# Sums of squares of norms: tiles added on GpSimd first, and summed over the partitions by TensorE once a norm

## The chip, the core and the metric

The kernel runs on one core of a Trainium2 chip. The metric is the device time of one execution in microseconds (us), as a median over runs. Engines are named as the profile names them: PE is TensorE (PEld its weight loads), DVE is VectorE, ACT is ScalarE, POOL is GpSimd, SP is SyncE, which issues most of the DMAs.

## What is computed

The reference is a network of two blocks over 256 tokens of 1024 features. The first block has a recurrent mixer (RWKV and S5) and a feed-forward. The second has two layers, each with gated linear attention, latent attention, a convolution module and a convolutional feed-forward; in its first layer 256 context tokens go along. What matters here are the norms between these parts:

```python
def _layer_norm(x, g, b):
    mu = x.mean(-1)
    var = ((x - mu) ** 2).mean(-1)
    return (x - mu) * rsqrt(var + eps) * g + b

def _rms_norm(x, g):
    return x * rsqrt((x * x).mean(-1) + eps) * g

x = _layer_norm(DN_ALPHA * x + gate1 * y, ln1_g, ln1_b)          # in every layer, for x and the context
h = silu(_layer_norm(_depthwise_conv(h), conv_ln_g, conv_ln_b))  # convolution module
of = of * rsqrt((of * of).mean(-1) + eps)                        # heads of the gated linear attention
cq, ckv = _rms_norm(pt[6], mla_q_norm), _rms_norm(pt[7], mla_kv_norm)   # latents
```

Each of them needs, for every token, a sum of squares over the features.

## The kernel before

**Layout.** Activations lie with their features on the partitions: a tensor of 1024 features is eight tiles [128 features, tokens], with 256 tokens, or 512 where the first layer of the second block takes x and the context together. So a sum over the features runs over the partitions and over the tiles. Weights are streamed from DRAM in pieces of 512 KB (`wraw`), and each is split into a high part `wh` (ACT, L275) and a low part `wl` (DVE, L276); a k-tile of a product is three matmuls (L311, L312, L313).

**Norms.** For each feature tile ACT squares it, and `colsum` takes the square as the stationary operand, 128 tokens at a time, against a column of ones: a matmul of 128x1 whose sums gather in PSUM (`pc`, in the buffers `aux`) over the tiles. In float32 each of these matmuls is two passes in the trace. `rms_of` then makes 1 / sqrt of the sums on DVE (L372 and eleven small instructions, tiles `rsv`, `rsw`, `rsy`) and spreads the result over the partitions with a transpose on PE (`rowcast`, L367). The places are these:

- Block 1: `post` twice (squares L542, of `b` tiles, as the tiles of a dense product come), and the norm ahead of the feed-forward (`squares`, L521).
- `ln`, six calls: for each feature tile DVE takes off the mean (L1104), ACT squares into an `lt` tile (four buffers, L1106). In layer 0 the norm after the mixer and that after the feed-forward are taken in two parts, of x and of the context; layer 1 has one after the mixer and the final one.
- `conv_norm`, one call a layer: tiles are fetched from DRAM (`od`) into `cv` buffers (two in layer 0, three in layer 1), the mean is taken off (L1406), squared in place (L1407). Its results `yc` (L306, L307) go into the products with `w_conv`.
- The heads of the gated linear attention, four a layer: two tiles each (`ring`, squares L1595).
- `latent`, four calls: two or three tiles each (`pr`).

**Order.** A framework of tiles allots the buffers and puts in the waits. A scheduler fixes the order of each engine's instructions when the program is built, from work that the code offers in steps (`beside()` and the generators of `dense_steps`); on the chip each engine goes through its own list in order. So PE's list mixes matmuls of products with column sums of a norm, and a column sum that isn't ready holds up what stands behind it. GpSimd does four memsets at the start and nothing else.

Of the kernel before, what the change touches and what calls it, by code (L numbers as in the profile page):

```python
# [21 lines left out]
P = 128  # L22
D = 1024
# [11 lines left out]
TAPS = ((5,), (1, 4))  # tiles whose taps the convolution takes at once  # L35
ADA = (17, 1, 1)  # chunks of the modulation beside the recurrence, the feed-forward and the inputs of the layers
# [3 lines left out]
# ------------------------------------------------------------------ host layout  # L40


class Weights:
    """Blocks [128, k-tiles * columns] of up to SPLIT elements a partition, one after the other in one flat array per weight."""
# [4 lines left out]
    def add(self, name, w, groups, moving=False):  # L49
        """w [K, N]; groups: column lists (-1: zeros), one chunk each; blocks of all columns (moving), else of whole tiles  # L50
        of 128 columns"""
# [30 lines left out]
class Vecs:  # L82
    """Per-feature vectors side by side: feature f of a vector -> partition f % 128, column f // 128."""
# [27 lines left out]
def actT(x):  # L111
    """[tokens, D] -> [128, D/128 * tokens]"""
    x = np.asarray(x)
    t, d = x.shape
    return np.ascontiguousarray(x.T.reshape(d // P, P, t).transpose(1, 0, 2).reshape(P, -1))
# [11 lines left out]
def const_arrays():  # L127
# [17 lines left out]
    # RWKV: rows j of a block of 64 steps, columns (a | r) of t  # L145
# [4 lines left out]
    # block levels of the triangular inverse, in A^T [j, t]: j in the even block, t in the odd one  # L150
# [7 lines left out]
    # rope  # L158
# [14 lines left out]
    # swap of the two halves of a 64-block; kr (64 rows) to both halves, straight and swapped  # L173
# [14 lines left out]
# ------------------------------------------------------------------ kernel body  # L188


class Body:
# [24 lines left out]
    def behind(self, work):  # L216
        """work(), whose VectorE instructions go before those of the block"""
# [14 lines left out]
    # ---- constants and vectors  # L232
# [15 lines left out]
    def v(self, which, name):  # L248
        """[128, tiles, L] view of a vector"""
        a, k, L = self.vat[which][name]  # L250
        return self.vt[which][:, a : a + k * L].rearrange("p (k l) -> p k l", l=L)
# [6 lines left out]
    # ---- weights: high and low parts, each exact in float32r  # L258
    def wraws(self, name, ch):
        """the blocks of a chunk as they come, [128, k, c]"""  # L260
# [6 lines left out]
    def wblocks(self, name, ch):  # L267
        """the blocks of a chunk, high and low parts as [128, k, c] each"""
# [10 lines left out]
    def wmoving(self, name, ch):  # L279
        """a chunk as k-tiles (wh, wl) of all its columns"""  # L280
# [4 lines left out]
    def wcols(self, name, ch):  # L285
        """tiles of 128 columns of a chunk, each as k-tiles (wh, wl)"""
# [7 lines left out]
    def split(self, pool, src, shape, tag):  # L294
        """src (float32, SBUF or PSUM) -> high and low parts"""
# [23 lines left out]
    def dense_steps(self, name, chunks, x, epi, tok=None, cuts=()):  # L319
        """epi(m, psum) for each tile m of 128 columns of the chunks, and what it returns one tile later; x: k-tiles  # L320
        [(xh, xl)]; tok: columns of x, by m"""
# [21 lines left out]
    # ---- 1 / sqrt(v), v > 0, small tiles: two steps of third order  # L343
# [14 lines left out]
    def colsum(self, pc, sq, first, last):  # L358
        """pc[:, t] += sum over the features of sq [128, tokens] of token tile t: tokens on partitions"""
# [4 lines left out]

    def rowcast(self, col, t, out):
        """out[p, i] = col[i, t] for every partition p"""
        self.nc.tensor.transpose(out, col[:, t : t + 1].broadcast_to([P, P]), self.ident)  # L367

    def rms_of(self, pc, ntt, dim, eps):
        """psum [128, tokens]: rsqrt(sum / dim + eps) of each token on every partition"""  # L370
# [8 lines left out]
    # ================================================================ block 1  # L379
    def block1(self, X, xp):  # L380
        """X [128, 8, 256], in place"""
# [3 lines left out]
        with ExitStack() as es:  # L385
            bp = es.enter_context(tc.tile_pool(name="b1", bufs=1))
            tp = es.enter_context(tc.tile_pool(name="b1t", bufs=2))
            # ---- pre norm
# [7 lines left out]
            with self.behind(lambda: R.append(self.rms_of(pc, 2, D, EPS))):  # L396
                hh, hl = self.rms_in(bp, X, "norm_mix_pre", R[0])
                # ---- vectors worked out on the chip
# [13 lines left out]
                # ---- projections: r, k, v, (wd | ad), gd with the token shift; u; gates  # L412
# [15 lines left out]
            # gates (twice the sigmoid less one), by way of DRAM  # L428
# [1504 lines left out]
```

## Time and profile before

| what | value |
|---|---|
| median of three runs | 2570.31 us (2566.24, 2570.31, 2585.77) |
| span of the profiled execution | 2588.6 us |
| PE busy | 2504.7 us, 97% |
| DVE, ACT, POOL busy | 1817.3, 1265.6 and 0.2 us (70%, 49%, 0%) |
| mean granted clock of TensorE | 0.971 |

The profiled execution took 18 us longer than the median; its rows give durations and order, and differences worked out from them are taken off the median. A start time in the trace is in us from the beginning of the span. A row of the timeline gives the start, the length, the engine, the line, the operation, the tile written and the tile read, how many instructions it stands for, and in brackets how long the engine had been idle and what ended that.

### The profile page before, as it was taken

The page shows a single profiled execution, that of the slowest core. Times are in us where ns is not written, and L with a number is a line of the kernel's source. Part 1 is how long each engine was busy: PE and PEld are TensorE (multiplying, and loading weights), DVE is VectorE, ACT ScalarE, POOL GpSimd, SP SyncE. Part 2 cuts the span into 40 slices and gives each one's busy share as a digit, 9 for nine tenths or more (in the row PEclk, how much of TensorE's full clock was granted, in tenths as well). Part 3 has the DMA queues.
Part 4 walks back from the last instruction along what each step waited for, and adds up shares of the span by engine and source line. Part 5 has one row for each costly group of instructions (what it writes and reads, how often), then busy time and mean ns, then how long its engine had stood idle before and what let it go on. Part 6 is the DMA issues. An engine that isn't in the chain of part 4 may idle for free.

```text
span 2588.6 us, 46013 instructions
## 1 busy us (share of the span) xinstructions
PE 2504.7 (97%) x18460; PEld 2153.4 (83%) x18460; DVE 1817.3 (70%) x3376; ACT 1265.6 (49%) x2264; POOL 0.2 (0%) x4
## 2 busy tenths in 40 slices
PE   7999998999999999999999999999989999998998
PEld 7587797997788888656888998899978887798998
DVE  8466367864596678778546875656787778877884
ACT  5432245654555542445433654444555545555653
POOL 0000000000000000000000000000000000000000
PEclk9799998999999999999999999999989999998998
DMA  6446565655331223342334452256542332365663
GB/s 212 159 135 234 196 188 172 187 178 170 111 101 52 77 74 97 122 140 87 114 114 154 148 172 97 96 167 186 161 125 87 99 122 80 115 195 164 190 197 111
DMA packets 125781, 361.53 MB, mean 140 GB/s; under 512 B 14208, under 2 KB 39680, under 8 KB 125440
## 3 DMA queue, kind: packets, MB, share of 16 engines
q1 hardware_dynamic: 125568, 358.59, 43.4%
q8 instruction: 145, 2.38, 0.4%
q14 instruction: 68, 0.56, 0.1%
HBM read 344.07 MB, written 14.46 MB: 139 GB/s over the span
## 4 chain that ended last, share of the span: by engine, by line
PE 88%; DVE 6%; ACT 2%; DMA 2%; issue 1%; SPq 0%; ACTq 0%; DVEq 0%
PE mm L311 21%; PE mm L312 21%; PE mm L313 21%; PE aux L362 2%; PE sy L1046 2%; DVE wl L276 2%; PE aux L1711 2%; PE aux L1592 1%; PE sy L1724 1%; PE aux L685 1%; PE aux L1710 1%; PE aux L1548 1%; PE mm L1513 1%; PE mm L1511 1%; PE mm L1512 1%
## 5 line engine op out<-in xcount | busy, mean ns | idle before, releaser
L275 ACT CAST wh<-wraw 128x1024 fp32r<-128x1024 f32 (+3 forms) x544 | 543.5, 1000 | 762.0 <-PE mm L312 640.3
L276 DVE TENSOR_TENSOR wl<-wraw,wh 128x1024 fp32r<-128x1024 f32 (+3 forms) x544 | 631.6, 1162 | 340.6 <-ACT wh L275 335.3
L311 PE MATMUL mm<-hx,wh 128*128 128x256 f32 (+1 forms) x1792 | 609.0, 340 | 13.7 <-ACT hx L303 6.4
L313 PE MATMUL mm<-hx,wl 128*128 128x256 f32 (+1 forms) x1792 | 603.6, 338 | 5.0 <-DVE wl L276 4.8
L312 PE MATMUL mm<-hx,wh 128*128 128x256 f32 (+1 forms) x1792 | 605.6, 339 | 0.2 <-DVE hx L304 0.2
L311 PEld LDWEIGHTS mm<-hx,wh 128*128 128x128 f32 x1792 | 343.1, 192 | 56.1 <-ACT hx L303 7.2
L313 PEld LDWEIGHTS mm<-hx,wl 128*128 128x128 f32 x1792 | 342.2, 191 | 44.5 <-DVE wl L276 6.9
L312 PEld LDWEIGHTS mm<-hx,wh 128*128 128x128 f32 x1792 | 343.3, 192 | 39.7 <-issue 4.7
L1393 DVE SCALAR_TENSOR_TENSOR cv<-u,h_conv_dw,cv 128x512 f32<-128x512 f32 (+1 forms) x480 | 295.2, 615 | 8.6
L311 PE MATMUL mm<-b,wh 128*128 128x256 f32 x688 | 199.5, 292 | 4.2 <-ACT b L303 3.6
L312 PE MATMUL mm<-b,wh 128*128 128x256 f32 x688 | 195.5, 285 | 1.0 <-DVE b L304 1.0
L313 PE MATMUL mm<-b,wl 128*128 128x256 f32 x688 | 195.5, 285 | 0.7 <-DVE wl L276 0.7
L312 PE MATMUL mm<-gx,wh 128*128 128x256 f32 x528 | 148.4, 281 | 0.0
L311 PE MATMUL mm<-gx,wh 128*128 128x256 f32 x528 | 147.8, 280 | 0.0
L313 PE MATMUL mm<-gx,wl 128*128 128x256 f32 x528 | 147.7, 280 | 0.0
L311 PEld LDWEIGHTS mm<-b,wh 128*128 128x128 f32 x688 | 130.8, 191 | 13.1 <-issue 5.3
L312 PE MATMUL mm<-sp,wh 128*128 128x256 f32 (+1 forms) x448 | 141.0, 315 | 0.1
L313 PE MATMUL mm<-sp,wl 128*128 128x256 f32 (+1 forms) x448 | 140.8, 315 | 0.1
L311 PE MATMUL mm<-sp,wh 128*128 128x256 f32 (+1 forms) x448 | 140.7, 315 | 0.0
L313 PEld LDWEIGHTS mm<-b,wl 128*128 128x128 f32 x688 | 131.2, 191 | 5.5 <-issue 2.5
L312 PEld LDWEIGHTS mm<-b,wh 128*128 128x128 f32 x688 | 131.6, 191 | 2.2 <-DVE b L304 1.7
L311 PEld LDWEIGHTS mm<-gx,wh 128*128 128x128 f32 x528 | 99.3, 188 | 0.0
(522 smaller groups left out, 4563.7 us busy)
## 6 DMA issues: line engine op xcount, KB each, us to landing
wraw<-w_up SPq DMA_DIRECT2D x100, 512.0 KB, 3.4
wraw<-w_ada SPq DMA_DIRECT2D x96, 512.0 KB, 4.3
wraw<-w_gates SPq DMA_DIRECT2D x48, 512.0 KB, 3.5
wraw<-w_dn SPq DMA_DIRECT2D x48, 512.0 KB, 3.7
wraw<-f_up SPq DMA_DIRECT2D x44, 512.0 KB, 3.5
wraw<-w_in SPq DMA_DIRECT2D x34, 512.0 KB, 4.1
wraw<-w_conv SPq DMA_DIRECT2D x32, 512.0 KB, 3.8
wraw<-w_o SPq DMA_DIRECT2D x24, 512.0 KB, 3.5
```

Source lines behind the costliest of these rows:

```text
L275: nc.scalar.copy(h, raw)
L276: nc.vector.tensor_tensor(l, raw, h.bitcast(F32), ALU.subtract)
L311: mm(ps, wh, xh, start=first, stop=False)
L312: mm(ps, wh, xl, start=False, stop=False)
L313: mm(ps, wl, xh, start=False, stop=last)
L362: self.nc.tensor.matmul(pc[:, t : t + 1], sq[:, t * P : t * P + P], self.ones[:, 0:1], start=first and t == 0, stop=last and t == n - 1)
L685: mm(ps[q, i], lhs(8 * b + i, q), rhs(8 * b + i, q), start=True, stop=True)
L1046: nc.tensor.matmul(ps[q], self.sc[:, 2 * k : 2 * k + 32], w[:, i], start=k < nt, stop=k >= KT - nt)
L1393: nc.vector.scalar_tensor_tensor(r(o), u[:, :, j : j + S], dw(j), r(o), ALU.mult, ALU.add)
L1511: mm(ps, xh[:, tk], wh, start=kk == 0, stop=False)
L1512: mm(ps, xl[:, tk], wh, start=False, stop=False)
L1711: mm(ps, qr[hs, a], kr[hs, k0:], start=False, stop=True)
```

## The change

A new helper `gather` adds a square to an accumulator with one elementwise instruction on GpSimd. `colsum` is then called once for a norm, on the sum of the tiles. In `squares` and `post` the accumulator is the first square's tile, in `ln` the first `lt` tile, in a head the first square; `conv_norm` gets a tile `acc` of its own in the pool `cp`, and `latent` one in buffers of the tag `vm`. The norm at the head of block 1 is as before.

```diff
+    def gather(self, acc, sq, first):
+        if first:
+            return sq
+        self.nc.gpsimd.tensor_tensor(acc, acc, sq, ALU.add)
+        return acc
...
     def squares(self, pc, X, sq, k):
         self.nc.scalar.activation(sq[:, k], X[:, k], AF.Square)
-        self.colsum(pc, sq[:, k], k == 0, k == KT - 1)
+        self.gather(sq[:, 0], sq[:, k], k == 0)
+        if k == KT - 1:
+            self.colsum(pc, sq[:, 0], True, True)
...
             nc.scalar.activation(sq[:, m], ps, AF.Square, scale=scale)
-            return lambda: self.colsum(pc, sq[:, m], m == 0, m == KT - 1)
+            self.gather(sq[:, 0], sq[:, m], m == 0)
+            if m == KT - 1:
+                return lambda: self.colsum(pc, sq[:, 0], True, True)
...
+        acc = None
         for k in range(KT):
             nc.vector.tensor_tensor(s[k], s[k], R, ALU.add)
             q = self.t(pool, [P, w], tag="lt", bufs=4)
             nc.scalar.activation(q, s[k], AF.Square)
-            self.colsum(pc, q, k == 0, k == KT - 1)
+            acc = self.gather(acc, q, k == 0)
+        self.colsum(pc, acc, True, True)
...
+        acc = self.t(cp, [P, W], tag="acc")
         for k in range(KT):
             o = tile()
             nc.sync.dma_start(o, od[k])
             nc.vector.tensor_tensor(o, o, R, ALU.add)
-            nc.scalar.activation(o, o, AF.Square)
-            self.colsum(pc, o, k == 0, k == KT - 1)
+            q = o if k else acc
+            nc.scalar.activation(q, o, AF.Square)
+            self.gather(acc, q, k == 0)
+        self.colsum(pc, acc, True, True)
...
-            for dv in range(2):
-                self.colsum(pc, sqs[dv], dv == 0, dv == 1)
+            self.colsum(pc, self.gather(*sqs, False), True, True)
...
+            acc = self.t(gp, [P, 4, S], tag="vm", bufs=2).rearrange("p a b -> p (a b)")[:, :w]
...
+                sq = sq if m else acc
                 nc.scalar.activation(sq, t, AF.Square)
                 raw.append(t)
-                return lambda: self.colsum(pc, sq, m == 0, m == kt - 1)
+                self.gather(acc, sq, m == 0)
+                if m == kt - 1:
+                    return lambda: self.colsum(pc, acc, True, True)
```

In all 212 of 276 column-sum matmuls go (two passes each): 28 in the two posts, 14 in the norm ahead of the feed-forward, 84 in the six `ln`, 42 in the two `conv_norm`, 24 in the heads, 20 in the latents. GpSimd gets 91 adds, 76 of 128x256 and 15 of 128x512. ACT, DVE and SP keep their instructions. Lines behind the helper stand 7 to 19 lines lower: L1106, L1407 and L1724 are L1117, L1422 and L1743 after the change.

PE's list in the first part of the norm after layer 0's mixer, before the change (`lt` are the squares, `aux` the sums, `sp` and `wh`, `wl` belong to a product that runs beside the norm):

```order
L312 MATMUL mm_13931<-sp_13531,wh_13927 128x256
L362 MATMUL aux_13833<-v_c_2_75,lt_13851 128x1 x2
L313 MATMUL mm_13931<-sp_13530,wl_13928 128x256
L311 MATMUL mm_13931<-sp_13530,wh_13927 128x256
L312 MATMUL mm_13931<-sp_13531,wh_13927 128x256
L362 MATMUL aux_13833<-v_c_2_75,lt_13856 128x1 x2
```

The same norm after the change:

```order
L311 MATMUL mm_13900<-sp_13470,wh_13896 128x256
L312 MATMUL mm_13900<-sp_13471,wh_13896 128x256
L313 MATMUL mm_13900<-sp_13470,wl_13897 128x256
L311 MATMUL mm_13900<-sp_13470,wh_13896 128x256
L362 MATMUL aux_13773<-v_c_2_75,lt_13776 128x1 x2
L312 MATMUL mm_13900<-sp_13471,wh_13896 128x256
```

The eight pairs have become one, behind 42 matmuls of the product since the mean (L1102), where the last of the eight stood behind 38. In the two parts of the norm after the feed-forward it is 40 for 36 and 45 for 40, in the heads of the linear attention 15 for 10 (layer 0) and 9 for 6 (layer 1), and none for none in the very last head.

ACT's list in the convolution's norm of layer 1, before the change (`cv` are its tiles, `PT`, `pr` and `sy` belong to the latent attention that ends here):

```order
L1407 ACTIVATE cv_22633<-cv_22633 128x256
L1718 ACTIVATE pr_22596,smx_22594<-aux_22590,mx_22593 128x512
L1176 ACTIVATE gate_22945<-mm_22920,h_b_gates_18007 128x256
L275 CAST wh_23015<-wraw_23013 128x1024
L1722 COPY PT_22573<-aux_22600 128x4x128
L1407 ACTIVATE cv_22639<-cv_22639 128x256
L303 CAST sp_21576<-sy_22572 128x256
L1407 ACTIVATE cv_22645<-cv_22645 128x256
```

And after it:

```order
L1741 COPY PT_22478<-aux_22505 128x4x128
L303 CAST sp_21481<-sy_22477 128x256
L1422 ACTIVATE acc_22526<-cv_22527 128x256
L275 CAST wh_22980<-wraw_22978 128x1024
L1189 ACTIVATE gate_22910<-mm_22885,h_b_gates_17926 128x256
L1422 ACTIVATE cv_22541<-cv_22541 128x256
```

The first square, which now writes `acc`, has moved behind the last L303 of the latent attention; the second and third still stand ahead of that. GpSimd's list around the same norm, after the change (there is nothing there before it; `vm` are the accumulators of two latents, `pr` their squares):

```order
L369 TENSOR_TENSOR vm_20705<-vm_20705,pr_20773 128x256
L369 TENSOR_TENSOR vm_20705<-vm_20705,pr_20809 128x256
L369 TENSOR_TENSOR vm_20822<-vm_20822,pr_20890 128x512
L369 TENSOR_TENSOR acc_22526<-acc_22526,cv_22531 128x256
L369 TENSOR_TENSOR acc_22526<-acc_22526,cv_22536 128x256
```

Five more with `acc` follow. Each add reads and writes its accumulator, so that of one norm no add can begin before the one ahead of it has ended, and PE's one pair of column sums waits for the last.

## Rows read from the trace of the kernel before

**Rows 1.** The page: busy time, and the shares of the chain that ended last.

```profile
PE 2504.7 (97%) x18460; PEld 2153.4 (83%) x18460; DVE 1817.3 (70%) x3376; ACT 1265.6 (49%) x2264; POOL 0.2 (0%) x4
...
PE 88%; DVE 6%; ACT 2%; DMA 2%; issue 1%; SPq 0%; ACTq 0%; DVEq 0%
```

**Rows 2.** The column sums' line (L362), those of `ln`: durations in ns, minimum/median/maximum.

```profile
L362 PE MATMUL aux<-v_c,lt x192: 164/250/353, 1424.9 to 2577.9; 128*128 128x1 f32 x192
```

**Rows 3.** Timeline of PE, first part of the norm after layer 0's mixer.

```profile
1428.77 0.28 PE L311 MATMUL mm<-sp,wh 128*128 128x256 f32 x1
1428.89 0.28 PE L312 MATMUL mm<-sp,wh 128*128 128x256 f32 x1
1429.01 0.50 PE L362 MATMUL aux<-v_c,lt 128*128 128x1 f32 x4
1429.37 0.36 PE L313 MATMUL mm<-sp,wl 128*128 128x256 f32 x1
1429.57 0.28 PE L311 MATMUL mm<-sp,wh 128*128 128x256 f32 x1
```

**Rows 4.** Groups by line and form on DVE: busy us, mean ns | idle before.

```profile
L276 DVE TENSOR_TENSOR wl<-wraw,wh 128x1024 fp32r<-128x1024 f32 x472 | 576.9, 1223 | 328.2 <-ACT wh L275 324.0 <-ACT att L1563 1.9
...
L1275 DVE TENSOR_TENSOR ring<-ring,ring 128x512 f32<-128x512 f32 x16 | 11.1, 692 | 0.5
L1247 DVE TENSOR_TENSOR lt<-lt,M 128x256 f32<-128x256 f32 x18 | 7.6, 424 | 0.4
```

**Rows 5.** Timeline of PE, behind the last column sums of a `post`.

```profile
396.62 1.92 PE L1046 MATMUL mm<-wraw,sc 128*32 128x512 f32 x14
```

**Rows 6.** Timeline of DVE, layer 0's convolution norm.

```profile
1249.31 0.69 DVE L1406 TENSOR_TENSOR cv<-cv,sx 128x512 f32<-128x512 f32 x1 [3.37 <-DMA cv<-od]
```

**Rows 7.** Timeline of layer 1's convolution norm, and of the products that take its results.

```profile
2264.34 0.35 ACT L303 CAST sp<-sy 128x256 fp32r<-128x256 f32 x1
...
2271.09 0.16 DVE L372 TENSOR_SCALAR rsv<-aux 128x2 f32<-128x2 f32 x1 [0.56 <-PE aux L362]
...
2318.81 0.28 PE L311 MATMUL mm<-yc,wh 128*128 128x256 f32 x1
...
2319.21 0.43 DVE L307 SCALAR_TENSOR_TENSOR yc<-cv,yc 128x256 fp32r<-128x256 f32 x1 [0.48 <-ACT yc L306]
```

**Rows 8.** Timeline of one head of the linear attention in layer 0, and one in layer 1.

```profile
781.05 0.61 ACT L1595 ACTIVATE ring<-aux 128x512 f32<-128x512 f32 x1
782.46 0.95 PE L362 MATMUL aux<-v_c,ring 128*128 128x1 f32 x8
...
1964.98 0.41 ACT L1595 ACTIVATE ring<-aux 128x256 f32<-128x256 f32 x1
...
1965.74 0.50 PE L362 MATMUL aux<-v_c,ring 128*128 128x1 f32 x4
```

**Rows 9.** Timeline of the first part of the norm after layer 0's mixer: third to seventh square, last column sum.

```profile
1426.73 1.79 ACT L1106 ACTIVATE lt<-M 128x256 f32<-128x256 f32 x5
...
1431.17 0.50 PE L362 MATMUL aux<-v_c,lt 128*128 128x1 f32 x4
```

**Rows 10.** Timeline of three norms: after layer 1's mixer, the final one, ahead of block 1's feed-forward.

```profile
2367.32 2.92 ACT L1106 ACTIVATE lt<-M 128x256 f32<-128x256 f32 x8 [1.62 <-DVE M L1104]
2367.79 4.91 PE L362 MATMUL aux<-v_c,lt 128*128 128x1 f32 x32 [1.33 <-ACT lt L1106]
2372.74 0.16 DVE L372 TENSOR_SCALAR rsv<-aux 128x2 f32<-128x2 f32 x1 [3.13 <-PE aux L362]
...
2570.88 1.88 ACT L1106 ACTIVATE lt<-ring 128x256 f32<-128x256 f32 x5 [9.25 <-DVE ring L1104]
2578.26 0.16 DVE L372 TENSOR_SCALAR rsv<-aux 128x2 f32<-128x2 f32 x1 [5.10 <-PE aux L362]
...
402.27 0.72 ACT L521 ACTIVATE b<-X 128x256 f32<-128x256 f32 x2
404.30 5.28 PE L362 MATMUL aux<-v_c,b 128*128 128x1 f32 x24 [0.51 <-ACT b L521]
409.62 0.16 DVE L372 TENSOR_SCALAR rsv<-aux 128x2 f32<-128x2 f32 x1 [1.96 <-PE aux L362]
```

## The prediction, made before the changed kernel was timed

> **What bounds the kernel now.** I read the page first: PE is busy 97% of the span, and 88% of the chain of waits runs over it [rows 1]. So a matmul taken off PE's list is worth its time wherever PE has other work at hand, and a wait put into that list costs its full length. Then the column sums' own line, which gives their number [rows 2]: 192 passes in the six `ln`, 552 in all by the same count, of which the change leaves 128. The duration printed there (250 ns median) is no price, since matmuls overlap. The price comes from the timeline, where the column sums stand in a row of matmuls: from one L312 to the L311 behind it 0.68 us pass, with four passes and two other matmuls (L312 and L313) in between; two matmuls in a row without column sums are 0.12 us apart. So four passes, a 256-wide tile, add 0.68 − 2 × 0.118 = 0.445 us, 0.111 us a pass, and a 512-wide tile 0.89 [rows 3]. All 424 passes that go are worth 424 × 0.111 = 47 us, 1.8% of the span. This is the ceiling; the question is what the adds on GpSimd give back.
>
> **The price of an add.** No row of before has an elementwise operation on GpSimd. I bound it by DVE's. The same form, float32 with two inputs, takes DVE 0.424 us at 128x256 and 0.692 at 128x512; the nearest row above is 1.223 us for 128x1024, four times the columns [rows 4]. With 0.05 us for the hand-over to the next instruction, the time p from one 256-wide add to the next is between 0.47 (GpSimd as quick as DVE) and 1.27 (it takes for 256 columns what DVE takes for 1024). For 512 columns I call it q: 0.75 to 2.1. I take p = 0.85 and q = 1.4, twice DVE's rows, the middle, because neither end has a row nearer to it. The Trainium skill, page "GPSIMD Engine Reference", section 3.1 (side-by-side cycle accounting), gives a GpSimd add 1.96 times VectorE's time, and section 4.1 puts elementwise adds on VectorE; an estimate by its ratio would be 0.83 and 1.36 without hand-over, and the sum about 2 us less than mine. No run of before shows either.
>
> **Part by part** (gains positive; in brackets the value at the low and at the high end of p). In each norm the adds form a chain, since each reads and writes the accumulator.
>
> *Posts*: two norms, seven tiles' column sums less in each: 2 × 7 × 0.445 = **+6.2** [+6.2, +6.2]. Squares come at the pace of a dense product, slower than the adds at either end, and behind the last square PE still has 14 passes of L1046, 1.92 us, to do [rows 5], which cover the last add.
>
> *Latents*: layer 0 loses three 512-wide tiles, layer 1 two of 256 and one of 512: 4 × 0.89 + 2 × 0.445 = **+4.5** [+4.5, +2.5]. The column sum is queued one tile of the product later, some 24 matmuls or 2.8 us, and square and add together take 0.6 + 1.4. At the high end 0.6 + 2.1 and the waits around them fill this, and up to 0.5 us each is lost.
>
> *Convolution, layer 0*: 7 × 0.89 = 6.2 less on PE. The tiles come through two buffers, which DVE waits for 3.37 us at a time for the load [rows 6]. A buffer is now freed by GpSimd's add and not by PE's, so its round is load 3.2, mean 0.69, square 0.63, add 1.4, together 5.9 us for two tiles, about the pace of before; I leave 1.7 us for PE at the one column sum that is left: **+4.6** [+6.2, +1.9].
>
> *Convolution, layer 1*: here a chain of other engines is late next. The last `yc` is there at 2319.64; PE begins on them at 2318.81 and needs the eighth tile 7 × 3 × 0.118 = 2.5 us later, at 2321.3 [rows 7]. So the norm may come 1.7 us later, no more. The first square writes `acc` and stands behind the L303 that ends at 2264.7; it ends at 2265.1. Its buffer then takes two more tiles (load 3.2, mean and square 0.85, add 0.85 each), the next buffer likewise one add later: the last add ends at 2275.9, and with the column sum and hand-overs L372 runs near 2276.9, 5.8 us after its 2271.09. PE then waits 5.8 − 1.7 = 4.1 us at its first products with `yc`; the 3.1 us of column sums saved earlier only make it wait sooner: **−4.1** [−2.8, −4.7]. If ACT's order were what it was, this term would be about zero.
>
> *Heads*: in layer 0 PE saves eight passes, 0.89 us, and has five more matmuls ahead of its column sum, so it arrives at 782.46 − 0.89 + 5 × 0.118 = 782.16; the second square ends at 781.66, the add 1.45 later at 783.11 [rows 8]. It waits 0.95 and has saved 0.89, four times. In layer 1 the same sum is: arrival 1965.74 − 0.445 + 3 × 0.118 = 1965.65, add done at 1966.27, a wait of 0.62 for 0.445 saved, three times; the last head has no matmul in between and loses 0.4 to 0.5. Together **−1.2** [+3.0, −5.7].
>
> *Three `ln` with a product beside them* (layer 0): 7 × 0.445 = 3.1 us less on PE each. In the one shown the third square is ready at 1427.1, and six adds follow it in a chain: 1427.15 + 6 × 0.85 = 1432.25. PE reaches its column sum at 1431.17 − 3.1 + 4 × 0.118 = 1428.55 [rows 9]. It waits 3.7 us for 3.1 saved; three such norms give 3 × −0.6 = **−1.8** [+4.8, −9.6].
>
> *Four bare norms*, where PE has little else to do and the next step is DVE's L372. In the one after layer 1's mixer the eight squares take 2.92 us and the 32 passes 4.91, so L372 runs at 2372.74. After: second square at 2368.1, seven adds 5.95, column sum and hand-over 0.55: 2374.6, or 1.85 later. The second part of the norm after layer 0's mixer goes alike: 2 × −1.85. In the final norm 32 passes take longer, L372 at 2578.26; after: 2571.65 + 5.95 + 0.85 = 2578.45, −0.2. Ahead of block 1's feed-forward 402.99 + 5.95 + 0.9 = 409.85 against 409.62, −0.2 [rows 10]. Together **−4.1** [+5.2, −15.9].
>
> ACT, DVE and SP keep their work; 91 adds are some 85 us of GpSimd's span, which has nothing else to do.
>
> The **sum**: 6.2 + 4.5 + 4.6 − 4.1 − 1.2 − 1.8 − 4.1 = +4.1 us at p = 0.85; with p at 0.47 it is +27, with p at 1.27 it is −25. So the sign turns near p = 0.91. Measured against the median of 2570.3, not against the profiled execution's 2588.6 us span, whose extra 18 us I can't place in any norm, the forecast is 2566 us. About 1%, 26 us, is what a measurement of this kernel can tell from no change; 4 us is inside.
>
> **The rivals.**
>
> (A) *The gain of PE shows in full as far as chains allow.* If an add takes what DVE's rows show, p = 0.47, all terms but layer 1's convolution are gains: +27, 2543 us. For it speaks that GpSimd has nothing else to do [rows 1]; against it that nothing here shows it to be as quick. One percent is reached below p = 0.5.
>
> (B) *The adds wait for DVE, and PE for the adds: slower than before.* DVE has an instruction with two inputs running most of the time: the split of the weights alone is 472 instructions of 1.223 us, 577 us of the span [rows 4], and it goes on beside the three `ln` and the convolution norms. If an add that arrives during one starts only behind it, p grows from 0.85 by up to 1.22, by 0.6 if it falls anywhere within. The place are PE's column sums in the `ln`, since seven adds follow each other there; at p = 1.27 the sum is −25, 2595 us, and every further 0.1 costs 7 us. It decides from p = 0.91 for the sign. In the bare norms DVE is free for most of the chain, and this speaks for a loss of half that. By the Trainium skill, page "SBUF — State Buffer", section "Who interferes with whom", a VectorE operation with two SBUF inputs and GpSimd exclude each other for the length of an instruction, by a lock on a shared port; the trace of before has no GpSimd instruction beside one of VectorE and shows nothing of it.
>
> (C) *The change doesn't do what it says.* The list of PE has the 212 matmuls fewer, so this is out but for a scheduler that fills the gaps otherwise; a percent at most.
>
> **How the numbers follow.** The forecast, p between 0.5 and 1.2 and little harm from DVE, 2550 to 2590 around 2566: 0.62. (A) 2540 to 2550: 0.12, all but a little of it over 1% faster. (B) from 2590 up, with its half form inside 1%: 0.24. (C) 0.02. The range 2543 to 2598 takes both ends of p and a few us beyond the high one; 2 in 10 stay outside, most of them above. Faster by over 1% is 0.12, as (A); slower by over 1% 0.17, the larger part of (B); the rest, 0.71, within.
>
> **What would show it.** In the profile after, L362 has 128 passes in place of 552. The add's line on GpSimd gives p: mean and pitch, alone (after layer 1's mixer) and beside DVE's L276; a mean that is longer there speaks for (B). PE's idle time ahead of L362 should name the adds and be near 3.7 us in the three `ln` with a product, 0.9 in the heads, none in posts and latents. L372 should run 1.9 us later after the mean in the bare norms. PE should wait some 4 us for `yc` in layer 1. The forecast is wrong if p is outside 0.5 to 1.2, if DVE's instructions grow longer beside the adds (then the weights' low parts come late, and PE waits for `wl`), or if the granted clock falls in PE's new waits and stays low behind them.

## The result, and the profile after

The changed kernel is slower: 2594.43 us against 2574.26 us (medians of 14 runs each), a ratio of 1.0070 with an interval of 1.0053 to 1.0088. By the ratio that is a loss of some 18 us where a gain of 4 was forecast; the time lies inside the stated range, on the other side of no change.

The page of the changed kernel, busy time by engine, to be read against [rows 1]:

```profile
PE 2450.2 (94%) x18036; PEld 2100.6 (81%) x18036; DVE 1823.4 (70%) x3376; ACT 1266.8 (49%) x2264; POOL 86.3 (3%) x95
```

PE has the 424 passes fewer and is busy 54 us less, 43 less than in a second profile of the kernel before that follows below (2493.3 us; the first had TensorE at half clock for a stretch). The time is longer all the same. So the work went, and waits came. The groups of the adds on GpSimd (busy us, mean ns | idle before and what ended it):

```profile
L369 POOL TENSOR_TENSOR lt<-lt,lt 128x256 f32<-128x256 f32 x42 | 33.8, 804 | 868.0 <-ACT lt L1118 865.3
L369 POOL TENSOR_TENSOR b<-b 128x256 f32<-128x256 f32 x21 | 18.8, 897 | 582.7 <-ACT b L551 573.0 <-ACT b L528 9.3
L369 POOL TENSOR_TENSOR acc<-acc,cv 128x512 f32<-128x512 f32 x7 | 10.6, 1512 | 290.0 <-ACT acc L1422 280.3 <-ACT cv L1422 9.5
...
L369 POOL TENSOR_TENSOR vm<-vm,pr 128x512 f32<-128x512 f32 x4 | 5.8, 1462 | 39.7 <-ACT pr L1658 39.7
L369 POOL TENSOR_TENSOR ring<-ring,ring 128x512 f32<-128x512 f32 x4 | 5.6, 1394 | 314.8 <-ACT ring L1611 314.8
```

The length of an add was taken well: 0.80 and 0.90 us for the two groups that hold 63 of the 76 adds of 256 columns, 1.39 to 1.51 for 512 (1.4 forecast). But the forecast's 0.85 is the time from one add to the next. Seven adds in a row behind layer 1's mixer, with little beside them, show 0.80 from start to start for 0.72 of length, so 0.08 lies between two adds:

```profile
2373.64 5.53 POOL L369 TENSOR_TENSOR lt<-lt,lt 128x256 f32<-128x256 f32 x7 [96.32 <-ACT lt L1118]
```

With these 0.08 the two groups stand at 0.88 and 0.98, about the 0.91 at which the forecast's sum turns from gain to loss. What PE waited for in the changed kernel (in all us, times, longest):

```profile
PE aux L362 <- POOL lt L369: 33.6, 6, 8.2
...
PE aux L362 <- POOL b L369: 10.2, 1, 10.2
...
PE aux L362 <- POOL acc L369: 7.2, 2, 3.9
PE aux L362 <- POOL ring L369: 6.9, 8, 1.5
...
PE aux L362 <- POOL vm L369: 2.9, 3, 1.1
```

Behind such a wait TensorE does not go on as before. Timeline of PE in the first part of the norm after layer 0's mixer, the place of [rows 3, 9]:

```profile
1424.30 1.01 PE L362 MATMUL aux<-v_c,lt 128*128 128x1 f32 x4 [3.83 <-POOL lt L369]
1425.17 0.56 PE L312 MATMUL mm<-sp,wh 128*128 128x256 f32 x1
1425.53 0.41 PE L313 MATMUL mm<-sp,wl 128*128 128x256 f32 x1
1425.74 0.41 PE L311 MATMUL mm<-sp,wh 128*128 128x256 f32 x1
...
1430.01 0.41 PE L313 MATMUL mm<-sp,wl 128*128 128x256 f32 x1
1430.22 0.35 PE L311 MATMUL mm<-sp,wh 128*128 128x256 f32 x1
1430.41 0.28 PE L312 MATMUL mm<-sp,wh 128*128 128x256 f32 x1
1430.53 0.28 PE L313 MATMUL mm<-sp,wl 128*128 128x256 f32 x1
```

The wait is 3.83 us, as forecast (3.7). Then for five us the matmuls stand 0.21 us apart where [rows 3] has 0.12. The granted clock was 0.50 in this stretch, the lower of its two levels (1.2 and 2.4 GHz) (the row gives us, busy time of the engines, then the granted clock and DMA):

```profile
1425.17:1430.22 5.05, 5.05 (x24) 5.05 (x25) 2.62 (x8) 0.61 (x1) 0.00 (x0) 0.50 0.32 103
```

Those 22 matmuls cost 2.1 us more than at full clock, and no term of the sum had them. (The second profile of the kernel before has 3.4 us at half clock in this norm too, so it is not among the extra losses counted at the end.) In the latents of layer 0 a wait of 1.15 us and the eight passes of the column sum stood ahead of the fall:

```profile
954.83 1.05 PE L362 MATMUL aux<-v_c,vm 128*128 128x1 f32 x8 [1.15 <-POOL vm L369]
955.75 0.64 PE L311 MATMUL mm<-hx,wh 128*128 128x512 f32 x1
956.18 0.63 PE L312 MATMUL mm<-hx,wh 128*128 128x512 f32 x1
...
959.71 0.39 PE L312 MATMUL mm<-hx,wh 128*128 128x512 f32 x1
959.94 0.39 PE L313 MATMUL mm<-hx,wl 128*128 128x512 f32 x1
```

Here the pitch is 0.43 in place of 0.23 us. The third thing to see is VectorE ahead of block 1's feed-forward (`X` is the residual, L561 its addition, in pairs; the first row is a pair of the kernel before, second profile, where it is L550, the others are of the changed kernel):

```profile
389.51 0.76 DVE L550 TENSOR_TENSOR X<-X,b 128x256 f32<-128x256 f32 x2
...
389.40 0.76 DVE L561 TENSOR_TENSOR X<-X,b 128x256 f32<-128x256 f32 x2
390.71 0.73 POOL L369 TENSOR_TENSOR b<-b 128x256 f32<-128x256 f32 x1 [7.53 <-ACT b L528]
390.85 1.21 DVE L561 TENSOR_TENSOR X<-X,b 128x256 f32<-128x256 f32 x2
392.31 3.26 POOL L369 TENSOR_TENSOR b<-b 128x256 f32<-128x256 f32 x4 [0.87 <-ACT b L528]
392.76 1.43 DVE L561 TENSOR_TENSOR X<-X,b 128x256 f32<-128x256 f32 x2
```

The pair takes 0.76 us before GpSimd has begun and 1.21 to 1.43 beside its adds. On GpSimd's side the same: an add of the first `post` takes 1.16 us where it begins during a weight split, and 0.74 where no split runs:

```profile
368.54 1.22 DVE L276 TENSOR_TENSOR wl<-wraw,wh 128x1024 fp32r<-128x1024 f32 x1 [1.37 <-ACT wh L275]
369.21 1.16 POOL L369 TENSOR_TENSOR b<-b 128x256 f32<-128x256 f32 x1 [1.43 <-ACT b L551]
...
379.64 0.74 POOL L369 TENSOR_TENSOR b<-b 128x256 f32<-128x256 f32 x1 [2.08 <-ACT b L551]
```

By the Trainium skill, page "SBUF — State Buffer", section "Who interferes with whom", a VectorE instruction with two inputs in SBUF (the memory that holds the tiles) and a GpSimd instruction that reads SBUF exclude each other. The trace agrees so far as that each is longer beside the other in these rows.

### The profile page after: what moved, and what is told of

It reads as the page before. It is cut to its first block, busy times and chain, and to the rows that moved or that the text cites. A ratio compares the mean times of both kernels' runs of the same rounds, so it can differ in the third digit from the quotient of the medians.

```text
span 2595.3 us, 45411 instructions
## 1 busy us (share of the span) xinstructions
PE 2450.2 (94%) x18036; PEld 2100.6 (81%) x18036; DVE 1823.4 (70%) x3376; ACT 1266.8 (49%) x2264; POOL 86.3 (3%) x95
## 5 line engine op out<-in xcount | busy, mean ns | idle before, releaser
L312 PE MATMUL mm<-sp,wh 128*128 128x256 f32 (+1 forms) x448 | 143.7, 321 | 0.1
L311 PE MATMUL mm<-sp,wh 128*128 128x256 f32 (+1 forms) x448 | 143.5, 321 | 0.0
```

Of the source, the lines that this page charges most:

```text
L311: mm(ps, wh, xh, start=first, stop=False)
L312: mm(ps, wh, xl, start=False, stop=False)
```

## The experiments

**A second profile of the kernel before.** No edit.

> The kernel before once more, for a second profile of it. The first had TensorE at half clock for 34 us near the start of block 1, where the two kernels do the same. If that was chance, the span is 2572 to 2580 us and the stretch from 80 to 115 us is at full clock; if it belongs to the kernel before, it is there again, and part of the loss seen behind it is made up by it.

The time was 2578.42 us (one run), the span 2576.3. The first profile's extra time at the start was chance: its 34 us at half clock, from 103.7 us on, are not in the second. Both have a shorter stretch at half clock ahead of that (the second 10 us from 81.0), so the whole of 80 to 115 us is not at full clock. The windows from 100 to 140 us of the first and of the second profile (columns as above):

```profile
100.00:140.00 40.00, 38.03 (x236) 24.69 (x237) 10.38 (x19) 15.09 (x28) 0.00 (x0) 0.57 0.35 119
```

```profile
100.00:140.00 40.00, 38.00 (x382) 28.10 (x376) 19.46 (x36) 20.07 (x38) 0.00 (x0) 1.00 0.41 136
```

So the second profile is what the others are held against. For every instruction of PE that two kernels share I took the difference of its start times; what that difference grows by from one place to the next is the loss there. This table is worked out so (us, positive: later than the kernel before; the start, where the norms of all are alike, shows how much is chance; the columns are the changed kernel and five of the experiments below):

```
place                     changed  on DVE  idle adds  acc moved  DVE twice  short adds
start to first post          4.2     1.1      2.8        4.4        0.9       12.0
first post                  -2.7    -3.6     -0.2       -2.6       -3.3       -2.9
ahead of feed-forward        3.7     0.1      3.0        3.5        4.1        0.9
second post, end of block 1 -1.5    -1.2      0.9       -0.5       -1.2       -2.1
heads, layer 0               2.0    -2.4      2.0        3.2       -2.2       -0.5
latents, layer 0             3.2    -2.0      0.7        3.2       -3.1       -1.7
convolution, layer 0        -0.6    -6.1      1.0       -2.8       -6.0       -1.7
norm after mixer, layer 0    0.6    -4.5     -1.1       -0.6        1.4       -4.4
after feed-forward, first    2.7    -3.1      0.3        1.4       -2.9       -1.9
after feed-forward, second   2.1     1.4     -1.2        2.2        6.3        0.0
heads, layer 1               1.3    -0.7      0.7        1.6       -0.5        0.2
latents, layer 1            -3.1    -4.5     -2.9       -3.1       -4.4       -4.0
convolution, layer 1         7.0     2.7      0.3        0.2       -1.3       -2.9
norm after mixer, layer 1    1.2     0.4      1.8        1.1        3.2       -1.0
```

Stretches without norms are left out; they differ by 0.7 us at most but for 990 to 1190 us, where the doubled adds on VectorE show −2.5. The second profile itself had a half-clock stretch at the latents of layer 1 (2.2 us); 2 to 3 of the gain that all columns show there is that.

**The old column sums in `ln`.**

```diff
-            acc = self.gather(acc, q, k == 0)
-        self.colsum(pc, acc, True, True)
+            self.colsum(pc, q, k == 0, k == KT - 1)
```

> The changed kernel with the old column sums in the six ln alone. By the traces the six norms lost about 10 us together (3.1, 1.0, 2.7, 2.0, 1.2 and 0.1). If the loss sits at the norms where PE waits for the chain of adds, this gives 2582 to 2586 us, ratio to before 1.004. If it comes from GpSimd's adds slowing VectorE all over the kernel, the time stays above 2590 us.

Measured: 2589.35 us, ratio 1.0040 (1.0018 to 1.0062). By ratio that is some 8 us less than the changed kernel (1.0070), near the 10 expected, the median above the window; the two intervals overlap, so the 8 are rough. Less than half of the loss is in these six norms; the rest stays.

**PE kept busy in the wait.** Columns of `pc` behind the real ones take the old column sums, and nobody reads them:

```diff
             acc = self.gather(acc, q, k == 0)
-        self.colsum(pc, acc, True, True)
+            if k:
+                self.colsum(idle, q, k == 1, False)
+        self.colsum(pc, acc, False, True)
```

> The changed kernel, with the old column sums put back into the six ln as idle work (into columns of PSUM that nobody reads) beside the adds; the one real column sum still waits for the last add. Theory 1 (the new wait lets TensorE's clock fall, and the matmuls behind it run at half speed for some us): in the three norms with a product beside them PE waits at most 1.5 us, the granted clock stays at full, and each gets 1.5 to 2.5 us back although PE has 56 passes more: 2587 to 2590 us. Theory 2 (the wait for the adds is the whole loss; VectorE and GpSimd slow each other): PE's work only fills the wait, and the time is that of the changed kernel, 2593 to 2597 us.

Measured: 2595.90 us, ratio 1.0071 (1.0044 to 1.0097). In time my theory of the clock alone failed. In place it holds in part. The windows of ten us from the real column sum of the first part of the norm after the feed-forward, of the changed kernel and of this one:

```profile
1779.00:1789.00 10.00, 9.94 (x60) 9.94 (x61) 5.89 (x19) 1.89 (x2) 0.00 (x1) 0.68 0.30 93
```

```profile
1775.00:1785.00 10.00, 9.68 (x83) 9.30 (x81) 4.90 (x15) 3.29 (x6) 4.31 (x5) 1.00 0.32 92
```

With PE fed the clock stays full, and this norm loses 0.5 us in place of 2.7. But the second part lost as before (2.4 for 2.1), the norm after the mixer lost 2.0 for 0.6, and heads, latents and convolutions were not fed at all. The fed passes are work as well: PE has 168 passes more, some 19 us by the forecast's price, where the waits were.

**The adds on VectorE.**

```diff
-        self.nc.gpsimd.tensor_tensor(acc, acc, sq, ALU.add)
+        self.nc.vector.tensor_tensor(acc, acc, sq, ALU.add)
```

> The changed kernel with every add on VectorE in place of GpSimd. An add is 0.42 us here and none runs beside a VectorE instruction. Theory 1: the chains end sooner, PE's waits are under 2 us, the clock mostly stays: 2572 to 2582 us. Theory 2 gives the same or better, 2565 to 2578 us, since nothing is slowed. Rival (VectorE has no room: the adds stand behind weight splits of 1.2 us and push later splits back): 2595 us or more, with longer waits of PE for wl.

Measured: 2558.16 us, ratio 0.9922 (0.9894 to 0.9951): some 20 us faster than the kernel before, 38 than the changed one. The rival fell: VectorE has room for 91 adds. The idea of the change, fewer passes on PE, was good; the engine was not. The scheduler also puts PE's column sum elsewhere: in the dense norms behind 62, 68 and 86 matmuls, where it has 42, 40 and 45 for GpSimd, though GpSimd's add takes longer. So engine, length of an add and place of the column sum changed together here; the runs below take the length apart.

**Adds that nobody waits for.** The kernel before, and behind each column sum but a norm's first:

```diff
+    def idle(self, sq, first):
+        if not first:
+            self.nc.gpsimd.tensor_tensor(sq, sq, sq, ALU.add)
```

> The kernel before, with its column sums, and beside them the same number of GpSimd adds that nobody waits for: each adds a tile of squares to itself once TensorE has read it. Theory 2 (GpSimd and VectorE slow each other, and this is the loss): 2588 to 2596 us. Theory 1 with the wait (the loss comes from what waits for the end of the adds): 2574 to 2580 us, within what tells nothing from the kernel before.

Measured: 2586.78 us, ratio 1.0055 (1.0035 to 1.0075), 14 us lost by the ratio. Theory 2 holds so far: nothing waits for a sum here, PE's list is that of the kernel before but for a few places, and GpSimd's adds cost time through VectorE. But the time is not lost where the changed kernel loses it. An idle add begins when TensorE has read its square, so the last one of a norm runs beside VectorE's first small instructions of 1 / sqrt (L349, L351). These rows have the first of them (L349, 128x4), in the second profile of before, with idle adds, and in the changed kernel:

```profile
L349 DVE TENSOR_SCALAR rsy<-rsv 128x4 int32<-128x4 int32 x8 | 1.3, 167 | 0.1
```

```profile
L349 DVE TENSOR_SCALAR rsy<-rsv 128x4 int32<-128x4 int32 x8 | 4.7, 585 | 0.1
```

```profile
L349 DVE TENSOR_SCALAR rsy<-rsv 128x4 int32<-128x4 int32 x8 | 1.3, 165 | 0.1
```

PE waits for 1 / sqrt 9.6 us longer with the idle adds, about all that this trace loses against the second profile (8.5 us), and no longer for the squares, although ACT waits 11 us for buffers that the idle adds hold. The rows are of the second profile and of the run with idle adds:

```profile
PE aux L367 <- DVE rsy L355: 13.5, 7, 5.9
...
PE aux L362 <- ACT lt L1106: 3.7, 3, 1.4
```

```profile
PE aux L371 <- DVE rsy L355: 23.1, 17, 8.6
...
PE aux L362 <- ACT lt L1111: 3.6, 3, 1.4
```

In the changed kernel the last add of a norm is over before the column sum, and 1 / sqrt is as quick as before. So this run shows what GpSimd's adds can do to VectorE; it is no measure of what they did in the changed kernel.

**The same idle adds, an eighth as long or less.**

```diff
-            self.nc.gpsimd.tensor_tensor(sq, sq, sq, ALU.add)
+            self.nc.gpsimd.tensor_tensor(sq[:, :32], sq[:, :32], sq[:, :32], ALU.add)
```

> The kernel before with the idle adds of GpSimd cut to 32 of 256 or 512 columns: the same instructions, waits and buffers, an eighth of the work or less. If the idle adds cost 12 to 14 us because of their length beside VectorE, this gives 2574 to 2578 us. If their waits and the buffers that they hold are what costs, it stays at 2582 us or more.

Measured: 2576.09 us, ratio 1.0005 (0.9989 to 1.0022): nothing. So the hand-overs between the engines cost nothing, the length of the adds does. L349 (128x4) is back at 167 ns and PE's wait for 1 / sqrt at 13.8 us. An `lt` add of either run, full and cut (busy us, mean ns):

```profile
L367 POOL TENSOR_TENSOR lt<-lt 128x256 f32<-128x256 f32 x42 | 28.8, 690 | 872.3 <-PE aux L362 710.1 <-ACT lt L1111 161.5
```

```profile
L367 POOL TENSOR_TENSOR lt<-lt 128x32 f32<-128x32 f32 x42 | 11.3, 270 | 884.7 <-PE aux L362 884.7
```

A longer add also holds its buffer longer; by the waits above that did not reach PE.

**A link of the chain as long as GpSimd's, on VectorE.**

```diff
+        self.nc.vector.tensor_tensor(acc, acc, sq, ALU.add)
+        self.nc.vector.tensor_tensor(acc, acc, sq, ALU.max)
```

> Every add on VectorE, and behind each a maximum of accumulator and square, which changes nothing, so that a link of the chain takes about 0.80 us, as long as GpSimd's. If the length of the chain is what costs (whatever the engine), this gives back what VectorE won: 2585 to 2600 us. If GpSimd beside VectorE is what costs, it stays near the version with one add on VectorE, 2558 to 2570 us.

Measured: 2573.32 us, ratio 0.9995 (0.9979 to 1.0011), between the two theories. The length of a link takes back 19 of VectorE's 20 us, though the scheduler moved the column sums back with it (118, 111 and 86 matmuls in the dense norms). The largest losses stand in the second part of the norm after layer 0's feed-forward (+6.3), ahead of block 1's feed-forward (+4.1) and after layer 1's mixer (+3.2). Another 19 us lie between this kernel and the changed one, at links of about the same length. They can't be put down to GpSimd beside VectorE alone, since the place of PE's column sum differs as well: in this kernel PE waits nothing at the column sums of the first two dense norms and at most 0.15 us at any in layer 0's heads, latents and convolution; the changed kernel waits 3.8 and 3.1 us in the two norms and 9.5 us in those others together. A later place with GpSimd's adds was tried in the norms of layer 0 alone (below).

**The convolution's accumulator in another pool.**

```diff
-        acc = self.t(cp, [P, W], tag="acc")
+        acc = self.t(self.bp, [P, W], tag="cvacc")
```

> The changed kernel with the accumulator of the convolution's norm in another pool, so that ACT's first square no longer stands behind the end of the latent attention. If the place of this square is what made layer 1's convolution lose 7 us, PE's 3.3 us wait at the column sum, the half clock behind it and the 2.5 us wait for yc shrink, and the time is 2588 to 2590 us. If the chain of seven adds by itself is late, it stays at 2592 to 2595 us, with the column sum's wait still over 2 us.

Measured: 2583.63 us, ratio 1.0033 (1.0016 to 1.0051), some 10 us below the changed kernel. Rows of ACT, GpSimd and PE in layer 1's convolution norm, of the changed kernel and then of this one:

```profile
2264.97 0.37 ACT L303 CAST sp<-sy 128x256 fp32r<-128x256 f32 x1 [2.14 <-PE sy L1743]
2265.24 0.42 ACT L1422 ACTIVATE acc<-cv 128x256 f32<-128x256 f32 x1
...
2265.80 1.55 POOL L369 TENSOR_TENSOR acc<-acc,cv 128x256 f32<-128x256 f32 x2 [162.88 <-DVE sp L304]
...
2277.38 1.01 PE L362 MATMUL aux<-v_c,acc 128*128 128x1 f32 x4 [3.33 <-POOL acc L369]
```

```profile
2252.63 0.41 ACT L1422 ACTIVATE cvacc<-cv 128x256 f32<-128x256 f32 x1
2253.59 0.40 ACT L1422 ACTIVATE cv<-cv 128x256 f32<-128x256 f32 x1
2254.07 0.73 POOL L369 TENSOR_TENSOR cvacc<-cvacc,cv 128x256 f32<-128x256 f32 x1 [152.49 <-ACT cv L1422]
```

The first square ran some 12 us sooner, and layer 1's convolution lost 0.2 us in place of 7.0. The order of ACT was the cause, as the prediction had it.

**Both edits, VectorE and the other pool.** The accumulator and the adds as in the two diffs above:

```diff
+        acc = self.t(self.bp, [P, W], tag="cvacc")
...
+        self.nc.vector.tensor_tensor(acc, acc, sq, ALU.add)
```

> Adds on VectorE and the accumulator of the convolution's norm in the other pool, as a candidate for the best version. The traces leave 1 to 3 us in layer 1's convolution: 2554 to 2558 us, ratio to before 0.991. If VectorE's own queue sets the norm's end there, it is the same as with VectorE alone, 2558 us.

Measured: 2558.12 us, ratio 0.9935 (0.9917 to 0.9954), the same as VectorE alone: with short links the place of the first square does not matter.

**The column sums of `ln` later in PE's list.** With the other pool, `beside()` is called 4, 1, 1 and 4 times ahead of the column sum in the four calls of layer 0, and the column sum is held behind what stands in the program before it:

```diff
+        late = (4, 1, 1, 4, 0, 0)[self.lns]
+        self.lns += 1
+        for _ in range(late):
+            beside()
+        self.colsum(pc, acc, True, True, pin=late > 0)
...
+            if pin and t == 0:
+                self.tc.keep_in_program_order(ins)
```

> The changed kernel with the accumulator of the convolution's norm in the other pool (2584 us so far), and PE's one column sum in three norms of layer 0 put later in its list: behind 86, 56 and 86 matmuls of the product beside it in place of 42, 40 and 45 (and 24 in place of none in the second part of the norm after the mixer). If PE's place in the queue is what the adds cost there, the 11 us of waits and the half clock behind them go, and the time is 2570 to 2577 us. If the norm's end then comes later and holds up what follows, or the adds' effect on VectorE is the loss, it stays at 2580 to 2586 us.

Measured: 2598.07 us, ratio 1.0092 (1.0078 to 1.0106): some 15 us worse than with the pool alone. What PE waited for longest in this kernel:

```profile
PE sx L1108 <- DVE cv L1414: 19.7, 2, 18.8
```

In the second part of the norm after the feed-forward the steps pulled ahead were the last there were; behind the norm PE had to wait 18.8 us for the next layer's convolution. The first part of the norm after the mixer gained 4 us.

**The same, but with the second part of the norm after the feed-forward left where it was.**

```diff
-        late = (4, 1, 1, 4, 0, 0)[self.lns]
+        late = (4, 1, 1, 0, 0, 0)[self.lns]
```

> As the run before with the later column sums, but in the second part of the norm after layer 0's feed-forward the column sum stays where the changed kernel has it (behind 45 matmuls): there the step that was pulled ahead of it left PE without work behind it, by the trace 19 us. If the waits of the other places are what the later position takes away, 2576 to 2581 us, 4 to 8 us under the version with the moved accumulator alone (2584 us). If the gain of the first part of the norm after the mixer (4 us in the trace) was chance, it is 2583 to 2586 us.

Measured: 2583.27 us, ratio 1.0021 (0.9999 to 1.0043), against 1.0033 for the pool alone. The wait of 18.8 us is gone; whether the other places gained is inside both intervals. This is inconclusive.

**Short adds in the changed kernel.** This kernel leaves out most features from the sums of most tokens; it serves for its time alone.

```diff
-        self.nc.gpsimd.tensor_tensor(acc, acc, sq, ALU.add)
+        self.nc.gpsimd.tensor_tensor(acc[:, :32], acc[:, :32], sq[:, :32], ALU.add)
```

> The changed kernel with each add cut to 32 of 256 or 512 columns (the sums of squares leave out most of the features for the other tokens): the order of the instructions is nearly the same (PE's column sums stand a few matmuls earlier), the chains, waits and hand-overs are those of the changed kernel, but a link is short and the adds hold nothing up for long. If the length of the adds (as a wait and beside VectorE) is what turned the gain into a loss, this gains about what the adds on VectorE gain, 2550 to 2562 us, layer 1's convolution apart. If the order, the pools or GpSimd's hand-overs cost, it is 2580 us or more.

Measured: 2554.40 us, ratio 0.9907 (0.9884 to 0.9931), 24 us faster than the kernel before. The same chains, pools and hand-overs give the whole gain when a link is short, layer 1's convolution included. A short add shortens PE's wait and its effect on VectorE together, so this run bounds the two and does not part them. PE's waits for `lt` in it, to be read against 33.6 us above:

```profile
PE aux L362 <- POOL lt L369: 16.6, 6, 5.1
```

**The best version.** Adds on VectorE, and the old column sums in four of the six `ln`:

```diff
+            if self.lns in (0, 2):
+                acc = self.gather(acc, q, k == 0)
+            else:
+                self.colsum(pc, q, k == 0, k == KT - 1)
```

> Adds on VectorE, and in four of the six ln, those with little or nothing beside them, the old column sums. By the traces of the version with all adds on VectorE these four lost 2 to 3 us together. So 2554 to 2558 us, ratio to before 0.991 to 0.993; if the four chains were covered anyway it is the same as with VectorE throughout, 2558 us.

Measured: 2554.90 us, ratio 0.9910 (0.9878 to 0.9942). It beats both kernels; against VectorE throughout (0.9922) the intervals overlap, though in the trace the norms after layer 0's feed-forward and layer 1's mixer are better by 2 to 3 us.

## Why the prediction was wrong

Forecast and measured gain by place (us, positive: gain), the measured ones from the column "changed" of the table, 20 us less in all; its start is chance and is left out:

| place | forecast | measured |
|---|---|---|
| posts | +6.2 | +4.2 |
| latents | +4.5 | −0.1 (2 to 3 of it chance) |
| convolution, layer 0 | +4.6 | +0.6 |
| convolution, layer 1 | −4.1 | −7.0 |
| heads | −1.2 | −3.3 |
| six `ln` | −5.7 | −6.6 |
| ahead of the feed-forward | −0.2 | −3.7 |

**What held.** The ceiling, 47 us of passes. The mechanism of the six `ln`: PE's waits in the three dense norms (11.1 us forecast; 3.8, 3.1 and 4.3 measured). PE's waits in the heads (some 6.5 forecast, 6.9 measured). The wait in layer 1's convolution through ACT's order, though its size was 7.0 us for 4.1. The length of an add, nearly: with the 0.08 us between two adds it is about 0.91 on average where 0.85 was taken, and by the forecast's own sum this is the 4 us of gain. By the Trainium skill's ratio of 1.96 ("GPSIMD Engine Reference", section 3.1) an estimate of the length would be 0.83 and 1.36; alone the trace has 0.72 for 0.424, a ratio of 1.7. And the sum at a link as long as VectorE's, which was rival A: 27 us of gain forecast, 20 measured with the adds on VectorE, where the column sums stand later too. That the time fell inside the range is no merit of the sum: the upper end stands for adds of 1.27 us, and they took 0.9.

**The step that failed** is the price of a new wait. The sum takes a wait of PE for its length alone and lets the matmuls behind it go on 0.118 us apart; the clock, which the prediction names among what would make it wrong, has no term. Counted by the matmuls that stand at twice the pitch, more than in the second profile of before, the half clock costs 1.6 us in the heads of layer 0, 3.2 in its latents, 1.6 in its convolution, 2.2 in the first part of the norm after the feed-forward and 2.6 in layer 1's convolution, about 11 us together (elsewhere it is 3 to 4 us less, most of that the second profile's own stretch at the latents of layer 1). This is a count in one trace. Two runs bear it out: with PE fed in the wait, 2.2 us come back in the one place of the five that was fed, and with short adds only layer 0's convolution, where a wait of 2.9 us is left, still has such a stretch among the five.

**Some waits were also taken too low.** In the latents the forecast has none, and PE waited 2.9 us; in layer 0's convolution 1.7, and it waited 3.9. With the clock this turned +4.5 and +4.6 into −0.1 and +0.6.

**"ACT, DVE and SP keep their work; 91 adds are some 85 us of GpSimd's span, which has nothing else to do"** failed as well: it is true of the number of instructions, not of their length. In the changed kernel 16 instructions of VectorE are longer than before by more than 0.1 us, 8.8 us together. Only ahead of block 1's feed-forward can they be followed to PE: there the X additions end 1.7 us later after their first, and L372 stands 10.4 us behind the first of them in place of 8.4. That is 2.0 of the 3.7 us lost there. It is rival B's mechanism, but not its price or its place: I let it act through a longer p in the `ln`. The 14 us of the idle adds are not part of this loss. They lie behind L372, at 1 / sqrt: ahead of the feed-forward L372 comes as soon as before in that run (8.5 us after the first X addition), and the last instruction of 1 / sqrt (L355) begins 8.3 us behind it in place of 5.6.

The half clock, the two waits and the place ahead of the feed-forward make up about 20 us, the size of the miss; why the posts fall 2 us short is not known. This is worked out from traces, and the effects overlap, since an add that VectorE holds up ends later, and so does PE's wait and what follows it. What is shown by a run is the sum of all: with short adds everything that the change brings besides gives 24 us, so the whole loss is the length of the adds. How it divides between PE's early column sums, the clock behind them and VectorE stays open.

## What to carry to other kernels

Work moved to an idle engine is not free when its instructions and those of a busy engine make each other longer: test it first by adding the work idle, with nobody waiting, and again cut short. Then look in the trace which instructions waited, for idle work can hold up others than the real change does, as it did here. A chain that ends in a single instruction of the bounding engine must be shorter than the work queued ahead of that instruction; here the scheduler put that instruction earlier for the slower engine than for the quicker one. Price a new wait on TensorE at its length and, by the five places here, 1.6 to 3.2 us more for the slow matmuls behind it.

## What the runs showed of the hardware that I had not expected

A pair of VectorE's additions of 128x256, 0.76 us otherwise, took 1.21 to 1.43 beside GpSimd's adds, and a GpSimd add of 0.72 us took 1.16 where it began during a weight split. VectorE's smallest instructions are held up too: L349 on 128x4, 0.17 us, took 0.59 on average with idle adds beside it. In the latents TensorE's granted clock fell to 0.50 behind a wait of only 1.15 us and eight passes of column sums, and the matmuls stood at twice the pitch for 3.4 us; behind the wait of 3.83 us they did so for about five. An add of 32 columns on GpSimd still takes 0.27 us, where 256 take 0.69.
